# RWKV units that prepare both quarters ahead of the chain: what moves in a hybrid decoder step

## The chip, the cores and the metric

The kernel runs on one core of a Trainium2 chip. The metric is the device time of one execution in microseconds (us). Before the change it is 1862.17 us, the median of three runs (1860.52 to 1864.99). A difference under 0.2%, about 4 us, can't be told from no change.

## The reference, cut to what matters

One decoder layer runs for a prompt of 1024 tokens and for 8 samples of 8 tokens, 1088 columns in all; the model width is 1024. All is fp32. `h = RMSNorm(x)` is projected by one wide matrix; its columns feed sliding-window attention (branch A), RWKV-7 time mixing (branch B), two SiLU gates and two sigmoid merge gates. Each branch is gated and projected, the two are merged, projected again and added to `x`, and a last RMSNorm follows. Branch B is a recurrence over tokens, for 16 heads of 64:

```python
def step(S, inp):
    rt, wt, kt, vt, at, bt = inp
    sa = jnp.einsum('bhvk,bhk->bhv', S, at)
    S = S * wt[:, :, None, :] + sa[..., None] * bt[:, :, None, :] + vt[..., None] * kt[:, :, None, :]
    return S, jnp.einsum('bhvk,bhk->bhv', S, rt)
# r receptance, w decay = exp(-exp(-softplus(-(w0 + tanh(wl) @ w2)) - 0.5)), k key, v value,
# a = -kk (removal key), b = kk * sigmoid(a0 + al @ a2), kk = normalised k * k_k
```

Its output is normalised per head, gets the bonus `sum(r * k * r_k) * v`, and is gated.

## The kernel before

**Dense tiles.** The 93 weight tiles of 1024x128 are matrices of fp32 split into two fp32r parts (hi and lo). A dense tile is three products (hi by hi, hi by lo, lo by hi) over 8 row blocks and 3 column chunks (364, 364, 360), 72 matmuls that all have line L110 in the profile. PSUM results leave by ACT, DVE and POOL, most to DRAM.

**Stages.** `start` norms `x` and does the first three tiles (low-rank input, first gate, first key tile); PE, SP and POOL keep the program's order there. `rwkv` runs branch B with 56 dense tiles as filler; only PE's order is kept by hand there, the other engines' order is set by a scheduler with priorities (chain 400000, fronts 200000, inversion 0). `attention` and `final` follow.

**Order by a planner.** `drive` holds several streams, each a generator whose steps issue instructions. A stream yields how long it wants to wait on the planner's clock, counted in us of PE work, or the name of a mark that another stream sets. The stream that is due first goes next, and dense tiles, which never wait, fill the rest. So PE's order is fixed when the program is built. Due times are constants: WI (38.0) from the end of a front to its merge, WD (3.5) from a prefetch to its matmuls, WB from there to the bonus, WA ahead of later scores, WM, WH and WS in merge and chain.

**RWKV units.** Branch B is cut into 16 units: 4 pairs of head groups (two heads each), and 4 quarters of 256 tokens, the last with the 64 sample columns too. Within a quarter there are 4 chunks of 64 tokens. A unit `s` passes through:

- `front(s)`: for each of two groups `prefetch` (loads, L578) and `quarter` (L597): low-rank matmuls `lo`, decays `Pp` and their inverse (L650 to L653), normalised keys `kkn`, the products `RA` (receptances and removal keys, L669, L670) and `KB` (L678), the bonus (L682 to L688). The first group then waits for the mark `c{s-2}`, since some tiles have two buffers. Copies of `RA` go to `am` (DVE, L728) and `r0` (ACT, L729), the score matmuls `A` follow, then masked copies, `ab`, and transposes of `KB` and `zv`. The second group starts only then.
- `invert` (L764): the triangular systems go through DRAM to `TM`, and 31 steps of two DVE operations (`Tt` L784, `TR` L786) invert 32x32 blocks.
- `merge(s)` (matmuls `q_`): waits for `f{s}` plus WI, for the chain `c{s-1}` and the post `p{s-2}`; it fills the single tile `ti`.
- `chain(s)`: for each chunk three dependent matmul steps (PSUM tile `c`), whose results are copied half by ACT and half by DVE (`xs` L860 and L861, `vsu` L865 and L866), and the state update L877.
- `posts` and `samples` use what the chain leaves.

Of the kernel before, what the change touches and what calls it, by code (L numbers as in the profile page):

```python
# [14 lines left out]
P = 128  # L15
# [9 lines left out]
HD = 64  # L25
# [15 lines left out]
WI, WD, WB, WA, WM, WH, WS, WP, WT = 38.0, 3.5, 15.0, 0.8, 5.0, 1.4, 2.4, 5.0, 10.0  # L41
# [40 lines left out]
class Prog:  # L82
# [162 lines left out]
    def run(self):  # L245
        tc, nc = self.tc, self.nc
        nc.scalar.preload_act_table_set("natural_log_exp_and_others")
        with ExitStack() as top:
# [13 lines left out]
            self.d_l = dt([P, 2, NT], F32, name="d_l")  # L262
            self.d_s = [dt([P, NT], F32, name=f"d_s{m}") for m in range(NQS)]
# [17 lines left out]
    def start(self, xp, w0):  # L281

        nc, ep, prm, prd = self.nc, self.ep, self.prm, self.prd
        ones = xp.tile([P, P], F32, name="ones")
# [96 lines left out]
        go(tg)  # L381
        go(tk)
# [88 lines left out]
    def lora(self, c0, c1, z):  # L471
        nc, ep = self.nc, self.ep
        n = c1 - c0
        t = ep.tile([P, 364], F32, tag="zz", name=f"tl{c0}", bufs=2)
        self.sig_neg(t[0:64, :n], t[0:64, :n], z[0:64, :n], -2.0, 0.0)
        nc.vector.tensor_scalar(t[0:64, :n], t[0:64, :n], 2.0, -1.0, ALU.mult, ALU.add)
        zs = ep.tile([P, 2, 364], F32R, tag="zl", name=f"zs{c0}", bufs=1)
        for j, src in enumerate((t[0:64, :n], z[64:128, :n])):
            hi, lo = (slice(0, 64), slice(64, 128))[::1 - 2 * j]
            nc.scalar.activation(zs[hi, j, :n], src, AF.Copy)  # L480
            nc.vector.tensor_tensor(zs[lo, j, :n], src, zs[hi, j, :n].bitcast(F32), ALU.subtract)
        nc.sync.dma_start(self.d_l[:, :, c0:c1], zs[:, :, :n].bitcast(F32))

    def rwkv(self):
# [71 lines left out]
    def front(self, s):  # L556
# [16 lines left out]
        self.mark(f"f{s}")  # L573

# [3 lines left out]
    def prefetch(self, g, q):  # L578
# [3 lines left out]
        if g % 2 == 0:  # L582
            self.zl = ep.tile([P, 2, 364], F32R, tag="zl", name=f"zl{nm}", bufs=1)
# [8 lines left out]
        kkn = ep.tile([P, 320], F32, tag="kkn", name=f"kkn_{nm}", bufs=1)  # L592
# [4 lines left out]
    def quarter(self, g, q, gi, f):  # L597
# [9 lines left out]
        def v64(t):  # L607
            return t[:, :256].rearrange("p (c s) -> p c s", c=4)

        def s64(t):  # L610
            return t[:, 256:320].rearrange("p (b s) -> p b s", b=NB)

        def d64(t, off, w=64):
            return t[:, :260].rearrange("p (c s) -> p c s", c=4)[:, :, off:off + w]

        def d8(t, off, w=8):
            return t[:, 260:332].rearrange("p (b s) -> p b s", b=NB)[:, :, off:off + w]

# [4 lines left out]
        zr, zv = E("zr"), ep.tile([P, 5, 2, HD], F32, tag="zv", name=f"zv_{nm}", bufs=1)  # L623
# [7 lines left out]
        for j in range(2):  # L631
            t = E("e1", 2)
            ps = pl[j]
            self.mm(ps[:, :n], lhsT=w2[0][:, j, :], rhs=self.zl[:, j, :n], start=True, stop=False)
            self.mm(ps[:, :n], lhsT=w2[1][:, j, :], rhs=self.zl[:, j, :n], start=False, stop=True)
# [6 lines left out]
        nc.vector.memset(d64(sg, 0, 1), 0.0)  # L642
        nc.scalar.activation(d64(sg, 1), v64(res[0]), AF.Exp, scale=-1.0)
        if smp:
            nc.vector.memset(d8(sg, 0, 1), 0.0)
            nc.scalar.activation(d8(sg, 1), s64(res[0]), AF.Exp, scale=-1.0)
# [4 lines left out]
        Pp = E("Pp", 1, 332)  # L651
# [12 lines left out]
        RA = ep.tile([P, 5, 2, HD], F32, tag="RA", name=f"RA{nm}", bufs=1)  # L664
        KB = ep.tile([P, 5, 2, HD], F32, tag="KB", name=f"KB{nm}", bufs=1)

        def o8(t, j):
            return t[:, 4, j, :].rearrange("p (b s) -> p b s", b=NB)
        nc.vector.tensor_tensor(RA[:, :4, 0, :], v64(zr), d64(Pp, 1), ALU.mult)  # L669
        nc.vector.scalar_tensor_tensor(RA[:, :4, 1, :], v64(kkn), -1.0, d64(Pp, 0), ALU.mult, ALU.mult)  # L670
        if smp:
            nc.vector.tensor_tensor(o8(RA, 0), s64(zr), d8(Pp, 1), ALU.mult)
            nc.vector.scalar_tensor_tensor(o8(RA, 1), s64(kkn), -1.0, d8(Pp, 0), ALU.mult, ALU.mult)

        halves = [slice(h * 64, h * 64 + 64) for h in range(2)]
        for h, hr in enumerate(halves):
            for t, j in ((aa, h), (kf, 1 - h)):
                nc.vector.tensor_tensor(KB[hr, :4, j, :], v64(t)[hr], d64(Pi, 1)[hr], ALU.mult)  # L678
                if smp:
                    nc.vector.tensor_tensor(o8(KB, j)[hr], s64(t)[hr], d8(Pi, 1)[hr], ALU.mult)  # L680

        nc.vector.scalar_tensor_tensor(zr[:, :n], zr[:, :n], self.par(Q_RK + g), kf[:, :n], ALU.mult, ALU.mult)  # L682
        parts = self.split(ep, zr[:, :n], n, f"b{nm}")
        yield None, WB, "m"
        ps = self.ps("m", f"bo{nm}")
        self.sum2(ps[:, :n], self.bone, parts)
        nc.vector.tensor_tensor(zr[:, :n].rearrange("p (c s) -> p c s", s=64), ps[:, :n].rearrange("p (c s) -> p c s", s=64), zv[:, :n // 64, 0, :], ALU.mult)
        nc.sync.dma_start(self.d_b[g][:, a0:a0 + n], zr[:, :n])  # L688
        gn, qn = (g + 1, q) if gi == 0 else (g - 1, q + 1) if q < 3 else (g + 1, 0)
        if gn < NG and self.zmark(gn, qn) in self.marks:  # L690
            self.prefetch(gn, qn)

        if gi == 0:
            if f["s"] > 1:
                yield f"c{f['s'] - 2}", 0.0
            f["ab"] = cp.tile([P, f["nh"], HD], F32, tag="ab", name=f"ab{nm}", bufs=2, padded_shape=[P, 10, HD])
            f["vsu"] = cp.tile([P, 4, 2, P], F32, tag="vsu", name=f"vsu{nm}", bufs=2)
            f["pc"] = cp.tile([P, 4, 2], F32, tag="pc", name=f"pc{nm}", bufs=2)
            self.mark(f"v{f['s']}")
        if smp and f["s"] > 4:  # L700
            yield f"p{f['s'] - 4}", 0.0
        ab = f["ab"]
        S = dict(am=cp.tile([P, 2, 4, 2, HD], F32, tag="am", name=f"am{nm}", bufs=4),
                 r0=self.r0s[2 * (f["s"] % 2) + gi], ti=self.ti[:, gi],
                 kbt=cp.tile([P, 4, P], F32, tag="kbt", name=f"kbt{nm}", bufs=4),
                 vsu=f["vsu"][:, :, gi, :])
        sets = [(S, 0, 4, 4 * gi)]
# [799 lines left out]
```

## Time and profile before

| | |
|---|---|
| median of three runs | 1862.17 us |
| the profiled execution | 1868.65 us |
| its span, first to last instruction | 1866.9 us |
| mean granted TensorE clock | 0.951 |
| busy: PE, weight load, DVE, ACT, POOL | 89%, 84%, 65%, 52%, 27% |

The span is what one execution took from its first instruction to its last. Busy times are unions of an engine's instructions; two engines can be busy at once, so they don't add up. The granted clock is TensorE's, as a share of full speed. A wait is idle time of an engine, put down to what ended it.

### The profile page before, as it was taken

Reading aid. Unit: us, or ns where it says so; the run is one execution under the profiler, and the core shown is the slowest. Engines: PE = TensorE matmul, PEld = TensorE weight load, DVE = VectorE, ACT = ScalarE, POOL = GpSimd, SP = SyncE. Lnnn points to the kernel's source line nnn. Section 1 sums busy time; section 2 is a strip of 40 time slices with the busy share of each in tenths; the row PEclk is TensorE's granted clock in tenths of the full one; section 3 lists DMA queues with packets and bytes.
Section 4 is the critical chain, followed back from the end, with each engine's and each line's share of the span. In section 5 each row is a group of like instructions: output and inputs, shape, how many; then the busy total and the mean of one; then the engine's idle time right before and its main releaser. Section 6 shows DMA issues by size and latency. Waiting matters only on the chain.

```text
span 1866.9 us, 33535 instructions
## 1 busy us (share of the span) xinstructions
PE 1662.3 (89%) x11744; PEld 1568.0 (84%) x11744; DVE 1213.3 (65%) x3563; ACT 965.9 (52%) x2494; POOL 498.9 (27%) x650
## 2 busy tenths in 40 slices
PE   5889889799788897898898898898799999999997
PEld 4889789788778896787898788897699899899997
DVE  6323767767766876869767868855466777554443
ACT  5445547446456574466576467453466765432332
POOL 5554334244244234324432223231200000000000
PEclk9999999899889998999999899999799999999999
DMA  4334334334334333233343244322521445374521
GB/s 165 125 94 123 97 104 118 102 92 119 93 97 112 97 113 107 83 104 113 95 127 113 81 110 132 96 83 69 159 75 57 125 126 151 107 240 139 191 90 60
DMA packets 208812, 209.32 MB, mean 112 GB/s; under 512 B 108452, under 2 KB 179732, under 8 KB 208612
## 3 DMA queue, kind: packets, MB, share of 16 engines
q1 hardware_dynamic: 193860, 157.03, 28.9%
q0 software_dynamic: 14784, 50.15, 8.4%
q8 instruction: 93, 1.52, 0.4%
q14 instruction: 75, 0.61, 0.1%
HBM read 144.01 MB, written 65.07 MB: 112 GB/s over the span
## 4 chain that ended last, share of the span: by engine, by line
PE 53%; DVE 25%; ACT 6%; DMA 6%; issue 5%; POOL 3%; SPq 1%; DVEq 0%; POOLq 0%; ACTq 0%
PE d L110 32%; DVE TR L786 6%; PE wo L110 5%; DVE Tt L784 5%; PE c L110 3%; DVE KB L678 2%; PE s L110 2%; PE o L110 2%; DVE vsu L877 2%; PE pt L108 1%; PE y L110 1%; PE A L110 1%; DMA TM<-s 1%; POOL wlo L171 1%; DMA wraw<-in_w 1%
## 5 line engine op out<-in xcount | busy, mean ns | idle before, releaser
L110 PE MATMUL d<-hhi,whi 128*128 128x364 f32 (+1 forms) x1656 | 585.7, 354 | 69.5 <-ACT zz L404 21.4
L110 PE MATMUL d<-hlo,whi 128*128 128x364 f32 (+1 forms) x1656 | 566.6, 342 | 7.9 <-DVE hlo L350 7.0
L110 PEld LDWEIGHTS d<-hhi,whi 128*128 128x128 f32 x1656 | 329.7, 199 | 83.0 <-ACT zz L404 23.8
L110 PEld LDWEIGHTS d<-hlo,whi 128*128 128x128 f32 x1656 | 329.7, 199 | 12.7 <-DVE hlo L350 9.6
L110 PE MATMUL d<-hhi,wlo 128*128 128x364 f32 (+1 forms) x1656 | 333.0, 339 | 0.0
L110 PEld LDWEIGHTS d<-hhi,wlo 128*128 128x128 f32 x1656 | 283.4, 194 | 2.6 <-issue 2.1
L171 POOL TENSOR_TENSOR wlo<-wraw,whi 128x1024 fp32r<-128x1024 f32 x56 | 135.4, 2418 | 199.5 <-PE d L110 90.4
L786 DVE TENSOR_TENSOR TR<-TR,Tt 96x90 f32<-96x90 f32 (+26 forms) x496 | 149.5, 302 | 11.9
L784 DVE TENSOR_TENSOR Tt<-TM,TR 96x90 f32<-96x90 f32 (+26 forms) x496 | 136.4, 275 | 14.9 <-DMA TM<-s 3.3
L170 ACT ACTIVATE whi<-wraw 128x1024 fp32r<-128x1024 f32 x90 | 95.1, 1057 | 80.0 <-PE d L110 52.6
L853 POOL TENSOR_TENSOR sp<-vsu,pc 64x128 f32<-64x128 f32 x128 | 55.9, 437 | 224.6 <-DVE vsu L877 218.9
L405 POOL TENSOR_TENSOR zz<-zz,pad 128x364 f32<-128x364 f32 (+1 forms) x75 | 73.4, 979 | 133.5 <-ACT zz L404 118.6
L1341 POOL TENSOR_TENSOR xr<-xr,frs 128x256 f32<-128x256 f32 x2 | 1.8, 933 | 342.1 <-ACT frs L1338 342.1
L877 DVE SCALAR_TENSOR_TENSOR vsu<-c,pc,sp 64x64 f32<-64x64 f32 x240 | 68.0, 283 | 16.9 <-PE c L110 12.3
L1080 ACT ACTIVATE sc<-sc,st 128x256 f32<-128x256 f32 (+1 forms) x128 | 62.1, 488 | 28.9 <-DVE st L1076 28.8
L678 DVE TENSOR_TENSOR KB<-e,sg 64x256 f32<-64x256 f32 x128 | 64.2, 512 | 1.2
L403 ACT ACTIVATE pad<-d,prm 128x364 f32<-128x364 f32 (+1 forms) x75 | 40.7, 543 | 45.8 <-PE d L110 39.1
L110 PEld LDWEIGHTS c<-xs,ti 128*128 128x128 f32 x256 | 38.4, 205 | 30.8 <-DVE xs L861 28.4
L110 PE MATMUL d<-yhi,whi 128*128 128x364 f32 (+1 forms) x192 | 63.9, 333 | 0.0
L110 PE MATMUL d<-ylo,whi 128*128 128x364 f32 (+1 forms) x192 | 63.8, 332 | 0.0
L110 PE MATMUL d<-oh,whi 128*128 128x364 f32 (+1 forms) x192 | 63.2, 329 | 0.0
L110 PE MATMUL d<-ol,whi 128*128 128x364 f32 (+1 forms) x192 | 62.9, 328 | 0.0
(334 smaller groups left out, 3686.8 us busy)
## 6 DMA issues: line engine op xcount, KB each, us to landing
wraw<-in_w POOLq DMA_DIRECT2D x56, 512.0 KB, 4.0
wraw<-in_w SPq DMA_DIRECT2D x37, 512.0 KB
d_z<-zz POOLq DMA_DIRECT2D x48, 182.0 KB, 2.3
zv<-d_z SPq DMA_DIRECT2D x48, 128.0 KB
d_m<-sp SPq DMA_DIRECT2D x32, 182.0 KB
TM<-s SPq DMA_DIRECT2D x72, 64.0 KB
stageo<-d_o SPq DMA_DIRECT2D x8, 544.0 KB
d_z<-zz POOLq DMA_DIRECT2D x24, 180.0 KB, 3.9
```

The costliest lines, as they stand in the source:

```text
L108: self.nc.tensor.transpose(out, lhsT, rhs)
L110: self.nc.tensor.matmul(out, lhsT=lhsT, rhs=rhs, **kw)
L170: nc.scalar.activation(hi, raw, AF.Copy)
L171: (nc.vector if self.dve_lo else nc.gpsimd).tensor_tensor(lo, raw, hi.bitcast(F32), ALU.subtract)
L403: nc.scalar.activation(pad[:, 1:1 + m], ps[:, :m], AF.Copy, scale=mu)
L405: nc.gpsimd.tensor_tensor(z[:, :m], z[:, :m], pad[:, 0:m], ALU.add)
L678: nc.vector.tensor_tensor(KB[hr, :4, j, :], v64(t)[hr], d64(Pi, 1)[hr], ALU.mult)
L784: nc.vector.tensor_tensor(tv, M[s // 16][:np_, s % 16:s % 16 + 1, s + 1:32].to_broadcast([np_, cc, w]), R[:np_, 0:cc, s:s + 1].to_broadcas ...
L786: nc.vector.tensor_tensor(R[:np_, 0:cc, s + 1:32], R[:np_, 0:cc, s + 1:32], tv, ALU.add)
L853: nc.gpsimd.tensor_tensor(sp[h], vsu[h, c, :, h], pc[h, c].unsqueeze(2).to_broadcast([64, 2, HD]), ALU.mult)
L877: nc.vector.scalar_tensor_tensor(dst, pn[h, i, h], pc[h, c, i:i + 1], sp[h, i], ALU.mult, ALU.add)
L1080: nc.scalar.activation(sc[k], sc[k], AF.Exp, bias=st[:, 0, k:k + 1], accum_out=st[:, 1, k:k + 1])
```

## The change

The wait for `c{s-2}` moves from the middle of the front to behind the preparation of both groups. `quarter` ends with `KB`; `bonus`, `arrays`, `scores` and `turn` become functions of their own, and bonus and transposes run behind the inversion's issue. Receptances and removal keys are written straight into a persistent tile `X` (four of them), from which scores and chain read, so that the copies to `am` and `r0` go. Split low-rank factors are made once in `start` and kept in DRAM (`d_c`); `lora` writes its two parts from two smaller tiles, by two DMAs. `TM`'s second half is narrower. The chain's copies are all on DVE. Planner constants: WB 15.0 to 4.0, WA 0.8 to 2.0, new WR 3.0 and WE 12.0. Tiles `xs` and `sp` of the chain have one buffer in place of two.

```diff
-WI, WD, WB, WA, WM, WH, WS, WP, WT = 38.0, 3.5, 15.0, 0.8, 5.0, 1.4, 2.4, 5.0, 10.0
+WI, WD, WB, WA, WM, WH, WS, WP, WT, WR, WE = 38.0, 3.5, 4.0, 2.0, 5.0, 1.4, 2.4, 5.0, 10.0, 3.0, 12.0
 ...  # start()
         self.pre[T_RKVG] = self.load_w(T_RKVG)
         go(tg)
+        for g in range(NG):
+            raw, hi, lo = (xp.tile([P, 364], F32, tag="sq", name=f"l{x}{g}", bufs=4)[:, :2 * P] for x in "rhl")
+            nc.sync.dma_start(raw, self.I["lora"][:, g].rearrange("p j c -> p (j c)"))
+            nc.scalar.activation(hi.bitcast(F32R), raw, AF.Copy)
+            nc.vector.tensor_tensor(lo.bitcast(F32R), raw, hi, ALU.subtract)
+            for x, t in enumerate((hi, lo)):
+                nc.sync.dma_start(self.d_c[:, g, x], t)
         go(tk)
 ...  # rwkv()
-        self.r0s = [cp.tile([P, 2, 4, HD], F32, name=f"r0{x}") for x in range(4)]
+        self.xs = [cp.tile([P, 4, 4, HD], F32, name=f"X{x}") for x in range(4)]
 ...  # front()
         for i in range(2):
             yield from self.quarter(2 * p + i, q, i, f)
+        self.mark(f"e{s}")
+        yield f"e{s}", WE
+        if s > 1:
+            yield f"c{s - 2}", 0.0
+        if q == 3 and s > 4:
+            yield f"p{s - 4}", 0.0
+        f["ab"] = ...   # and vsu, pc
+        self.mark(f"v{s}")
+        for i in range(2):
+            self.arrays(2 * p + i, q, i, f)
+        for i in range(2):
+            yield from self.scores(2 * p + i, q, i, f)
 ...  # s1 to DRAM
         with self.tc.high_priority(offset=INV):
             self.invert(nm, n2, f)
         self.mark(f"f{s}")
+        for i in range(2):
+            yield from self.bonus(2 * p + i, q, f["q"][i])
+            yield from self.turn(2 * p + i, q, f["q"][i])
+        self.mark(f"t{s}")
+        ...   # prefetch of the next unit's first quarter
 ...  # prefetch()
-        raw = ep.tile([P, 2, P], F32, tag="w2", name=f"w2_{nm}", bufs=1)
-        nc.sync.dma_start(raw, self.I["lora"][:, g])
-        w2 = [ep.tile([P, 2, P], F32R, tag=f"w2{x}", name=f"w2{x}_{nm}", bufs=1) for x in "hl"]
+        w2 = ep.tile([P, 2, 2, P], F32R, tag="w2", name=f"w2_{nm}", bufs=1)
+        nc.sync.dma_start(w2.bitcast(F32).rearrange("p x j c -> p x (j c)"), self.d_c[:, g])
-        nc.scalar.activation(w2[0], raw, AF.Copy)
-        nc.vector.tensor_tensor(w2[1], raw, w2[0].bitcast(F32), ALU.subtract)
 ...  # quarter(): zr, zv, kkn, Pp and KB get two buffers
-        nc.vector.tensor_tensor(RA[:, :4, 0, :], v64(zr), d64(Pp, 1), ALU.mult)
-        nc.vector.scalar_tensor_tensor(RA[:, :4, 1, :], v64(kkn), -1.0, d64(Pp, 0), ALU.mult, ALU.mult)
 ...  # after the bonus
-        if gi == 0:
-            if f["s"] > 1:
-                yield f"c{f['s'] - 2}", 0.0
-                nc.vector.tensor_copy(am[hr, 1, :, h], RA[hr, :4, 1, :])
-                nc.scalar.activation(X["r0"][hr, h], RA[hr, :4, 0, :], AF.Copy)
 ...  # the new functions, cut
+    def bonus(self, g, q, S):
+        parts = self.split(ep, zk[:, :n], n, f"b{g}_{q}")
+        yield None, WB if g % 2 else 0.0, "m"
+        ...   # sum2, times zv, d_b
+    def arrays(self, g, q, gi, f):
+        X = self.xs[2 * (f["s"] % 2) + gi]
+        for h, hr in enumerate(halves):
+            nc.vector.tensor_tensor(X[hr, :, h], self.v64(zr)[hr], self.d64(Pp, 1)[hr], ALU.mult)
+            nc.vector.scalar_tensor_tensor(X[hr, :, 2 + h], self.v64(kkn)[hr], -1.0, self.d64(Pp, 0)[hr], ALU.mult, ALU.mult)
+    def scores(self, g, q, gi, f):
+            yield WA if c0 or gi else WR
+            ...   # A matmuls, rhs X[hr, c, h::2, :]; ab first, then the masked copies
+    def turn(self, g, q, S):
+        ...   # the transposes of KB and zv, as before
 ...  # invert(): the second half of M holds 16 columns in place of 32
 ...  # chain()
+        yield f"t{s}", WH
         yield f"m{s}", WH
-            nc.scalar.activation(xs[hs[0]], px[hs[0], :, hs[0]], AF.Copy)
-            nc.vector.tensor_copy(xs[hs[1]], px[hs[1], :, hs[1]])
+            for h in hs:
+                nc.vector.tensor_copy(xs[h], px[h, :, h])
-            nc.scalar.activation(vsu[hs[0], c, :, hs[0]], pu[hs[0]], AF.Copy)
-            nc.vector.tensor_copy(vsu[hs[1], c, :, hs[1]], pu[hs[1]])
+            for h in hs:
+                nc.vector.tensor_copy(vsu[h, c, :, h], pu[h])
```

## Rows read from the trace of the kernel before

**Rows 1.** Busy time by stretch: us of each engine with instructions, granted clock, DMA.
```profile
200.00:1290.00 1090.00, 948.72 (x7105) 897.37 (x7105) 805.78 (x2461) 605.81 (x1611) 373.59 (x494) 0.94 0.37 104
1290.00:1340.00 50.00, 33.92 (x179) 28.17 (x178) 23.32 (x56) 18.06 (x46) 15.60 (x22) 0.74 0.31 91
1340.00:1867.00 527.00, 514.87 (x3542) 489.90 (x3540) 303.89 (x874) 242.00 (x606) 8.13 (x8) 0.99 0.40 126
```

**Rows 2.** Chain of work that ended last, whole span: shares by line.
```profile
PE d L110 32%; DVE TR L786 6%; PE wo L110 5%; DVE Tt L784 5%; PE c L110 3%; DVE KB L678 2%; PE s L110 2%; PE o L110 2%; DVE vsu L877 2%; PE pt L108 1%; PE y L110 1%; PE A L110 1%; DMA TM<-s 1%; POOL wlo L171 1%; DMA wraw<-in_w 1%
```

**Rows 3.** Timeline of unit 9 (start us, us, engine, line, operation): its steps only.
```profile
786.53 1.16 PE L110 MATMUL A<-RA,KB 64*128 64x128 f32 x16
...
817.93 1.16 PE L110 MATMUL A<-RA,KB 64*128 64x128 f32 x16
...
833.25 0.19 DVE L786 TENSOR_TENSOR TR<-TR,Tt 96x31 f32<-96x31 f32 x1
...
866.78 2.60 SPq L788 DMA_DIRECT2D s<-TR  x3
...
879.47 0.86 PE L110 MATMUL q_1a<-ab 32*32 32x32 f32 x32
...
884.41 0.61 PE L110 MATMUL c<-vsu,am 128*128 128x128 f32 x4
...
926.79 1.16 PE L110 MATMUL A<-RA,KB 64*128 64x128 f32 x16
```

**Rows 4.** PE's waits, 100 to 1320 us: total us, times, longest.
```profile
PE c L110 <- DVE xs L861: 22.3, 15, 4.0
PE d L110 <- ACT zz L404: 19.2, 7, 4.5
PE d L110 <- DVE gz L435: 17.0, 4, 8.8
PE c L110 <- DVE vsu L866: 15.7, 18, 2.6
PE d L110 <- ACT sho L414: 10.5, 6, 2.8
```

**Rows 5.** DVE groups, 200 to 1290 us: busy us, mean ns, idle before.
```profile
L861 DVE COPY xs<-c 64x128 f32<-64x128 f32 x60 | 17.7, 295 | 48.2 <-ACT xs L860 47.0
...
L866 DVE COPY vsu<-c 64x128 f32<-64x128 f32 x60 | 17.7, 295 | 23.9 <-ACT vsu L865 22.5
```

**Rows 6.** Single lines: ns of one, minimum, median and maximum.
```profile
L678 DVE TENSOR_TENSOR KB<-e,sg x128: 406/418/2823, 123.6 to 1221.0; 64x256 f32<-64x256 f32 x128
...
L728 DVE COPY am<-RA x64: 274/291/2944, 126.9 to 1224.8; 64x256 f32<-64x256 f32 x64
...
L729 ACT ACTIVATE r<-RA x64: 401/416/422, 123.3 to 1217.5; 64x256 f32<-64x256 f32 x64
...
L860 ACT ACTIVATE xs<-c x64: 253/272/274, 249.1 to 1313.3; 64x128 f32<-64x128 f32 x64
...
L590 ACT ACTIVATE w2h<-w x32: 399/403/419, 3.5 to 1167.5; 128x256 fp32r<-128x256 f32 x32
```

**Rows 7.** Start, timeline of SP, then ACT and PE.
```profile
73.98 0.33 SPq L436 DMA_DIRECT2D d_g<-gz  x1
...
75.08 0.60 SPq L584 DMA_DIRECT2D zl<-d_l  x1
...
76.85 0.48 SPq L455 DMA_DIRECT2D out_sk<-sp  x1
...
84.92 0.57 ACT L404 ACTIVATE zz<-d,prd 128x364 f32<-128x364 f32 x1 [2.06 <-DMA out_sk<-sp]
...
89.13 0.43 PE L110 MATMUL d<-hhi,whi 128*128 128x364 f32 x1 [2.92 <-ACT whi L170]
```

**Rows 8.** Pieces of the chain that ended last: start us, us, what.
```profile
0.75 2.75 DMA w<-in_lora
...
1334.61 4.49 DMA vT<-d_v
```

More of the change, by code (lines that the diff above doesn't have):

```diff
@@ L573, in front, with v64, s64, d64 @@
         self.mark(f"f{s}")
+        for i in range(2):
+            yield from self.bonus(2 * p + i, q, f["q"][i])
+            yield from self.turn(2 * p + i, q, f["q"][i])
+        self.mark(f"t{s}")
+        gn, qn = (2 * p, q + 1) if q < 3 else (2 * p + 2, 0)
+        if gn < NG and self.zmark(gn, qn) in self.marks:
+            self.prefetch(gn, qn)
+    @staticmethod
+    def v64(t):
+        return t[:, :256].rearrange("p (c s) -> p c s", c=4)
+    @staticmethod
+    def s64(t):
+        return t[:, 256:320].rearrange("p (b s) -> p b s", b=NB)
+    @staticmethod
+    def d64(t, off, w=64):
+        return t[:, :260].rearrange("p (c s) -> p c s", c=4)[:, :, off:off + w]
+    @staticmethod
+    def d8(t, off, w=8):
+        return t[:, 260:332].rearrange("p (b s) -> p b s", b=NB)[:, :, off:off + w]
+    @staticmethod
+    def o8(t, j):
+        return t[:, 4, j, :].rearrange("p (b s) -> p b s", b=NB)
     def zmark(self, g, q):
@@ L703, in quarter @@
[L703 to L707, printed above, removed]
+                    nc.vector.tensor_tensor(self.o8(KB, j)[hr], self.s64(t)[hr], self.d8(Pi, 1)[hr], ALU.mult)
+        nc.vector.scalar_tensor_tensor(zk[:, :n], zr[:, :n], self.par(Q_RK + g), kf[:, :n], ALU.mult, ALU.mult)
@@ L749, in quarter @@
                     nc.scalar.activation(abv, pv[hr, :cn, 64:128], AF.Copy)
+            for h, hr in enumerate(halves):
+                pv, vr = pvs[h], halves[1 - h]
+                am0 = S["smp"]["am"][:, 0, :, h] if c0 else S["am"][:, :, h]
+                am1 = S["smp"]["am"][vr, 1, :, h] if c0 else S["X"][vr, :, 2 + h]
+                nc.vector.tensor_tensor(am0, pv[:, :cn, 0:64], self.cst(mi, 64).unsqueeze(1).to_broadcast([P, cn, 64]), ALU.mult)
+                nc.vector.tensor_tensor(am1, pv[vr, :cn, 64:128],
+                                        self.cst(ms, 64, vr.start, vr.stop).unsqueeze(1).to_broadcast([64, cn, 64]), ALU.mult)
+    def turn(self, g, q, S):
+        nc = self.nc
+        nm = f"{g}_{q}"
+        ident = self.cst(C_ID, P)
+        halves = [slice(h * 64, h * 64 + 64) for h in range(2)]
+        sets = [(S, 0, 4)] + ([(S["smp"], 4, 1)] if q == 3 else [])
+        for Y, c0, cn in sets:
             yield None, 0.0, "m"
@@ L771, in invert @@
         np_ = 3 * nb
-        M = [ep.tile([P, 16, 32], F32, tag=f"TM{x}", name=f"TM{x}{nm}", bufs=1) for x in range(2)]
+        M = [ep.tile([P, 16, 32 - 16 * x], F32, tag=f"TM{x}", name=f"TM{x}{nm}", bufs=1) for x in range(2)]
         R = ep.tile([P, 11, 32], F32, tag="TR", name=f"TR{nm}", bufs=1)
@@ L870, in chain @@
             for i in range(2):
-                self.mm(psy[:, c % 2, i, :], lhsT=vsu[:, c, i, :], rhs=Q[i]["am"][:, 0, c].rearrange("p h s -> p (h s)"), start=False, stop=(c % 2 == 1 and i == 1))
+                self.mm(psy[:, c % 2, i, :], lhsT=vsu[:, c, i, :], rhs=Q[i]["am"][:, c].rearrange("p h s -> p (h s)"), start=False, stop=(c % 2 == 1 and i == 1))
             if c == 3 and not smp:
```

147 lines of the change are left out of this document (67 added, 80 removed).

## The prediction, as it went on record

> **What bounds the kernel now.** I read the busy time by stretch first [rows 1]. From 200 to 1290 us, the RWKV stage with dense tiles as filler, PE is busy 948.7 of 1090 us at a granted clock of 0.94; from 1340 on it is busy 514.9 of 527 at 0.99. The second stretch has little left to win. In the first, PE stands for 1090 - 948.7 = 141 us, and the clock takes about 948.7 x 0.06 = 57 us of the work: 198 us lost. Between them lie 50 us (1290 to 1340) with PE at 33.9 and a clock of 0.74: that is 33.9 x 0.74 = 25 us of work, so 25 us lost. The granted clock has two levels (1.2 and 2.4 GHz), and the three rows order it as they order PE's share of busy time: 0.74, 0.94, 0.99. So a wait of PE costs more than its own length.
>
> The chain of waits [rows 2] shows what the stage hangs on besides dense matmuls: the inversion on DVE (TR 6% and Tt 5% of the span). The timeline of one unit [rows 3] shows the loop these shares come from; its steps recur in all 16 units. The scores of the unit's first quarter start at 786.53, straight behind the matmuls of the chain two units back. Those of the second quarter start at 817.93: in between, the whole second quarter is prepared. The inversion runs from 833.25 to 866.78, the merge starts at 879.47, the chain at 884.41, and at 926.79 the next-but-one unit begins. The loop of two units is 140.3 us, and 817.93 + 1.16 - 786.53 = 32.6 of it lie between the two score blocks' ends.
>
> But PE follows an order written at build time, and dense tiles fill it. A shorter loop is worth only the time in which PE stands or is slow. So I also read who PE waits for [rows 4]: the chain's two copies (22.3 + 15.7 = 38.0 us) and, apart from the loop, the evacuation of dense tiles (19.2 + 17.0 + 10.5 = 46.7).
>
> **The change part by part.** The sum is made against the profiled execution's own 1868.65 us (span 1866.9), which lies 6.5 above the median of the runs, 1862.17.
>
> *Both quarters ahead of the wait (loop).* Behind the chain two units back now come only the products for both quarters: 8 of 64x256 on DVE at 0.418 [rows 6] = 3.3 us, then two score blocks of 1.16 with about 2 us around them: about 8 us where 32.6 stood. The loop falls from 140.3 to about 116, 17%. The PE work in it is 140.3 x (948.7 x 0.94 / 1090 = 0.82) = 115 us. So the new loop would be just as long as PE's own work, and PE could not run without any loss; not all of it comes back. Of the 198 us lost, 38 belong to the chain's copies and 47 to dense evacuation; 113 are left, the clock's share included. I take 40 us, a third of that; bounds 0 (dense work fills it anyway) and -113.
>
> *Chain's copies, all on DVE.* ACT copies one half and DVE the other, one behind the other: DVE stands 47.0 + 22.5 us for ACT before its own copy [rows 5]. One hop between engines goes, and 128 more copies of 0.295 = 38 us are laid on DVE, less than the 69.5 us that it stands today. I take half of PE's 38.0 us: -19. Bounds: -38, and +38 if each added copy stood on the path in full.
>
> *Dense evacuation.* ACT loses 128 copies of 0.272 = 35 us, 64 of 0.416 = 27 (r0), 24 of 0.403 = 10 (w2h) [rows 6]: 72 of 605.8 us in the stage [rows 1], 12%. I take 12% of the 46.7 us: -6; bounds 0 and -47.
>
> *Arrays.* The eight products per unit replace four of 128x256 and four copies of 0.291 [rows 6]; at the same 0.418 for a product (estimate: DVE's time follows the columns, 256 in both) that is 3.3 against 2.8 us, nothing on PE. Narrowing the second half of TM takes bytes from three of six loads; 0.
>
> *The tail.* With a shorter loop the RWKV units end while dense tiles are left, and the stretch 1290 to 1340 fills up. Of its 25 us I take 20, since the first load of the attention stage (4.49 us [rows 8]) still ends a wait. Bounds 0 and -25.
>
> *New waits.* (a) The score matmuls come 3 planned us (WR) behind the chain, the products take 3.3 on DVE after a queue: 1 us per unit, +16. (b) The second quarter's prefetch now stands 3.5 planned us (WD) ahead of its matmuls, and its two factors arrive in one load; the nearest load, of half the bytes, took 2.75 us [rows 8], so I take 0. Behind either wait stand all dense matmuls, in PE's order. Together +16; bounds 0 and +105 (the second rival).
>
> *The split of the low-rank factors, moved to the start.* This part speaks against the change. In program order SP gets 24 DMAs between the last gate DMA (73.98) and the spill's last three (the last at 76.85) [rows 7]. SP is one of the engines whose order is kept by hand there. For each of 8 groups it issues a load, then waits for ACT's copy and DVE's difference before it issues the two stores. A load took 2.75 us from issue to landing [rows 8], the copy 0.403, the difference about the same, two issues about 0.34 each (as the gate's 0.33): 2.75 + 0.40 + 0.42 + 0.68 = 4.2 us, 34 us in all. The spill's stores move from 76 to about 108. A zz buffer hangs on them: today ACT waits for out_sk's landing at 84.92 and PE stands until 89.13. After, PE would stand from about 86 to 112, 26 less the 2.9 that it stands today: 23; I take +22, since weights then lie ready behind it. Bounds: 0 (zl, a later DMA, passes at 75.08, so SP's order is not rigid for all) and +33.
>
> [...]
>
> Sum: -40 - 19 - 6 - 20 + 16 + 22 = -47; 1868.65 - 47 = 1821.7 for a profiled execution, and 6.5 less for the median: 1815.
>
> **The rivals.**
> *The loop turns into PE's time in full.* For it: the first scores follow the chain at once, so no other wait ends later there. PE then recovers 100 of the 113 us and no new wait shows: 1868.65 - 100 - 19 - 6 - 20 + 22 = 1745.7, or 1739. Against: DVE is busy 805.8 of 1090 us [rows 1], and in an 11% shorter stage it would be at 83%.
>
> *The inversion is late (slower).* The inversion has the lowest priority on DVE and will run beside the preparation of two quarters of the next unit in place of one; and the merge's mark now comes ahead of the transposes, while its planned distance of 38 us (WI) stays. One quarter's DVE work is 4 products of 0.418 at least and some ten operations of the same width: about 6 us. From scores to merge the trace has 879.47 - 817.93 = 61.5 us, against 38 + 5 planned. It decides from the point where the inverse lands later than PE's order puts the merge; then PE stands in front of it, with all dense matmuls behind. If that is 6.6 us in each unit, +105 take the place of the -40 and the +16: 1868.65 + 105 - 19 - 6 - 20 + 22 = 1950.7; since the merge also waits for the chain of the unit before (the code's second condition), part of it would be hidden; I price it at half, +53: 1898.7, or 1892. Against: where that chain ends last, the inversion has time to spare.
>
> *The loop is hidden anyway.* Dense tiles fill PE whatever the loop does; the named waits alone change: 1868.65 - 19 - 6 - 20 + 16 + 22 = 1861.7, or 1855. For it: the longest of PE's named waits are not for the inversion [rows 4].
>
> **How the numbers follow.** Forecast 0.50, full gain 0.17, inversion late 0.20, hidden 0.13. A difference under 0.2% (4 us) can't be told from none here. Forecast and full gain are faster but for 0.02 of the forecast that may end level; of the hidden case 0.07 is faster, 0.05 level and 0.01 slower. Faster 0.48 + 0.17 + 0.07 = 0.72; same 0.02 + 0.05 = 0.07; slower 0.20 + 0.01 = 0.21. The forecast's own range is 1785 to 1845. For 8 in 10 it reaches half into the outer rivals: 1745 to 1885.
>
> **What would show it.** Loop: the two score blocks of a unit a few us apart, and the same step two units on about 116 us later. Copies: no DVE wait for ACT at xs and vsu, PE's waits for them halved. Tail: no stretch with PE near 34 of 50 us between the stages. Start: SP with 24 DMAs in a row from 74 us, and PE standing for over 20 us at about 86. New waits: PE waiting for DVE's X ahead of the scores. The prediction fails if PE waits for the merge's operands in most units, if the granted clock in the stage falls below 0.94, or if PE is busy over 95% of it.

## The result, and the profile after

The changed kernel takes **1926.91 us** (median of four runs, 1925.88 to 1931.61), beside 1862.04 us for the kernel before: a ratio of **1.0351, 95% interval 1.0330 to 1.0373**. It is 65 us slower where 47 faster were forecast, and outside the range. The profiled execution takes 1925.88 us, 57.2 more than that of before.

Busy time by stretch of the changed kernel, columns as in [rows 1]:

```profile
100.00:150.00 50.00, 18.67 (x98) 18.36 (x99) 3.60 (x12) 11.11 (x26) 22.79 (x38) 0.66 0.38 122
200.00:1290.00 1090.00, 909.84 (x6753) 856.49 (x6754) 830.51 (x2563) 543.82 (x1390) 376.44 (x491) 0.91 0.37 101
1290.00:1340.00 50.00, 49.25 (x424) 47.07 (x423) 22.73 (x67) 17.37 (x43) 18.38 (x21) 1.00 0.33 99
1340.00:1924.00 584.00, 569.88 (x3871) 542.97 (x3869) 324.50 (x910) 269.68 (x659) 25.80 (x26) 0.99 0.41 128
```

The stretch between the stages is full: 49.25 x 1.00 us of work where [rows 1] had 33.9 x 0.74, so 24 us. Two places are lost: the start (PE at 18.67 of 50 us, against 44.84 before) and the RWKV stage (909.8 at 0.91, where [rows 1] had 948.7 at 0.94). The same stretch of the start in the kernel before:

```profile
100.00:150.00 50.00, 44.84 (x272) 43.63 (x271) 12.12 (x39) 21.98 (x56) 26.48 (x32) 0.97 0.34 101
```

The prediction's own sign of failure, a granted clock under 0.94 in the stage, has come up.

PE's waits of the changed kernel from 100 to 1400 us, as in [rows 4]:

```profile
PE d L110 <- DVE gz L444: 45.6, 6, 16.5
PE d L110 <- ACT whi L170: 38.8, 1, 38.8
PE c L110 <- DVE xs L910: 24.6, 17, 3.2
PE d L110 <- ACT sho L423: 20.3, 7, 10.4
PE c L110 <- DVE vsu L915: 20.3, 21, 3.3
...
PE A L110 <- DVE X L788: 8.6, 9, 3.8
PE lo L110 <- DMA w<-d_c: 6.8, 3, 4.4
```

There is a single wait of 38.8 us for weights in the start. The gate's product `gz` stands at 45.6 us where [rows 4] had 17.0. The waits for the chain's copies, all on DVE now, are no shorter than in [rows 4] (44.9 against 38.0).

The start of the changed kernel, to set beside [rows 7]: SP, then POOL, ACT and PE.

```profile
78.88 0.38 SPq L386 DMA_DIRECT2D lr<-in_lora  x1
...
115.90 0.33 SPq L390 DMA_DIRECT2D d_c<-ll  x1
...
117.92 0.14 POOL L754 MEMSET ams<- 64x64 f32 x1 [36.25 <-DMA d_c<-ll]
...
123.84 0.57 POOL L169 DMA_DIRECT2D wraw<-in_w  x1
...
128.40 1.06 ACT L170 ACTIVATE whi<-wraw 128x1024 fp32r<-128x1024 f32 x1 [2.46 <-DMA wraw<-in_w]
...
129.51 0.67 PE L110 MATMUL d<-hhi,whi 128*128 128x364 f32 x1 [38.81 <-ACT whi L170]
```

The block of 24 DMAs lasts 37 us (78.88 to 116.23), where 34 were worked out. The row to learn from is POOL's: its memset of `ams`, a tile of the next stage, waits 36.25 us for a store of the block to land. I read it so that this tile takes over memory of the block; e1, e2 and e5 below bear it out. POOL keeps the program's order, so the next weight load (123.84) stands behind the memset, and PE behind that.

Units 8 to 11 of the changed kernel, PE but for one row of the chain's last step (of unit 8); beside [rows 3]:

```profile
884.41 1.18 DVE L926 SCALAR_TENSOR_TENSOR vsu<-c,pc,sp 64x64 f32<-64x64 f32 x4
...
915.09 1.16 PE L110 MATMUL A<-X,KB 64*128 64x128 f32 x16
918.52 1.18 PE L110 MATMUL A<-X,KB 64*128 64x128 f32 x16
...
947.38 1.41 PE L110 MATMUL lo<-zl,w 128*128 128x320 f32 x4
...
980.87 1.16 PE L110 MATMUL A<-X,KB 64*128 64x128 f32 x16
```

The two score blocks of unit 10 lie 3.4 us apart, as meant. But they start 29.5 us after the chain two units back has ended (884.41 + 1.18), so that chain no longer sets them. What does is the front itself: 33.5 us from `lo` (947.38) to the scores, and 32.3 from the scores of one unit to the `lo` of the next, 65.8 in all. The fronts are one stream, so no part of it overlaps the next front. The last state update of all units (last start in these rows) comes 26.6 us later than before, first the kernel before, then the changed one:

```profile
L877 DVE SCALAR_TENSOR_TENSOR so<-c,pc,sp x16: 275/284/291, 495.3 to 1318.6; 64x64 f32<-64x64 f32 x16
```

```profile
L926 DVE SCALAR_TENSOR_TENSOR so<-c,pc,sp x16: 266/284/293, 523.2 to 1345.2; 64x64 f32<-64x64 f32 x16
```

One stretch of DVE ahead of those scores (start, length, operation), with ACT's last step for the gate, and PE at its end:

```profile
887.63 0.41 DVE L711 TENSOR_TENSOR KB<-e,sg 64x256 f32<-64x256 f32 x1
...
887.76 0.49 ACT L222 ACTIVATE gz<-gz 128x364 f32<-128x364 f32 x1
...
893.23 0.41 DVE L740 TENSOR_TENSOR X<-zr,Pp 64x256 f32<-64x256 f32 x1
...
897.22 1.52 DVE L711 TENSOR_TENSOR KB<-e,sg 64x256 f32<-64x256 f32 x4
...
900.73 0.53 DVE L444 TENSOR_TENSOR gz<-d,gz 128x364 f32<-128x364 f32 x1
...
901.32 0.67 PE L110 MATMUL d<-hhi,whi 128*128 128x364 f32 x1 [14.78 <-DVE gz L444]
```

From 884 to 900 DVE runs without a break: keys and products of both quarters (fronts have priority 200000), and between them the last steps of an inversion. The gate's product (dense, priority 0) is ready when ACT is done at 888.25 and runs at 900.73. The kernel gives dense tiles two PSUM buffers, so PE stands for 14.78 us. The Trainium skill says that the queues of ScalarE, VectorE and GpSimdE are strict FIFO ("PSUM — Partial Sum Buffer", section "Engine vs sequencer instructions"). This trace agrees: the product is served 12.5 us after it is ready, in the order that was built, though PE waits.

### The profile page after: what moved, and what is told of

The parts are those of the page before. It is cut to its first block, busy times and chain, and to the rows that moved or that the text cites. A ratio compares the mean times of both kernels' runs of the same rounds, so it can differ in the third digit from the quotient of the medians.

```text
span 1924.1 us, 33459 instructions
## 1 busy us (share of the span) xinstructions
PE 1665.7 (87%) x11744; PEld 1570.1 (82%) x11744; DVE 1239.1 (64%) x3667; ACT 911.9 (47%) x2270; POOL 510.8 (27%) x654
## 4 chain that ended last, share of the span: by engine, by line
PE 48%; DVE 27%; DMA 8%; issue 7%; ACT 4%; POOL 3%; SPq 2%; DVEq 0%; POOLq 0%; ACTq 0%
PE d L110 29%; DVE Tt L832 6%; DVE TR L834 5%; PE wo L110 5%; PE c L110 2%; DVE vsu L926 2%; PE s L110 2%; DVE KB L711 2%; PE A L110 2%; PE o L110 2%; DMA wraw<-in_w 2%; PE pt L108 1%; DMA TM<-s 1%; PE y L110 1%; DMA lr<-in_lora 1%
## 5 line engine op out<-in xcount | busy, mean ns | idle before, releaser
L110 PE MATMUL d<-hhi,wlo 128*128 128x364 f32 (+1 forms) x1656 | 339.4, 343 | 0.0
L110 PEld LDWEIGHTS d<-hhi,wlo 128*128 128x128 f32 x1656 | 287.5, 197 | 3.9 <-issue 2.9
L832 DVE TENSOR_TENSOR Tt<-TM,TR 96x90 f32<-96x90 f32 (+26 forms) x496 | 157.1, 317 | 23.1 <-DMA TM<-s 10.2
L834 DVE TENSOR_TENSOR TR<-TR,Tt 96x90 f32<-96x90 f32 (+26 forms) x496 | 135.6, 273 | 12.7
L902 POOL TENSOR_TENSOR sp<-vsu,pc 64x128 f32<-64x128 f32 x128 | 63.2, 494 | 236.8 <-DVE vsu L926 218.6
L110 PEld LDWEIGHTS c<-vsu,kbt 128*128 128x128 f32 x256 | 37.7, 202 | 30.0 <-DVE vsu L915 29.3
```

Source lines behind the costliest of these rows:

```text
L110: self.nc.tensor.matmul(out, lhsT=lhsT, rhs=rhs, **kw)
L832: nc.vector.tensor_tensor(tv, M[s // 16][:np_, s % 16:s % 16 + 1, s + 1 - 16 * (s // 16):].to_broadcast([np_, cc, w]), R[:np_, 0:cc, s:s + ...
L834: nc.vector.tensor_tensor(R[:np_, 0:cc, s + 1:32], R[:np_, 0:cc, s + 1:32], tv, ALU.add)
L902: nc.gpsimd.tensor_tensor(sp[h], vsu[h, c, :, h], pc[h, c].unsqueeze(2).to_broadcast([64, 2, HD]), ALU.mult)
```

## The experiments

Ratios are against runs of the kernel before, made beside each experiment. "The three-undone kernel" is e6.

**e1: the block in one piece.** One load, one copy, one difference, two stores over all 8 groups.

```diff
-        for g in range(NG):
-            raw, hi, lo = (xp.tile([P, 364], F32, tag="sq", ..., bufs=4)[:, :2 * P] for x in "rhl")
+        raw, hi, lo = (xp.tile([P, KT, 364], F32, tag="xt", ..., bufs=3)[:, :, :2 * P] for x in "rhl")
```

> The kernel after, with the split of the low-rank factors in the start done once over all 8 groups (one load, one ACT copy, one DVE difference, two stores) in place of 8 times in turn. Theory A (the block of 24 DMAs costs the start's 39 us): PE's stand of 38.8 us before 129.5 us falls to some 8, and the time to 1890 to 1897. Rival (the start's delay is made up later by dense work that waits anyway, all of the loss lies in the RWKV stage): 1915 to 1927.

Measured 1911.33 us, 1.0263 (1.0243 to 1.0282): 15.6 less. PE's stand falls from 38.8 to 17.2 us, not to 8, and the time lies above the theory's range. The stand is the block's, but POOL still waits 15.0 us for its last store.

**e2: the same 24 DMAs behind the key tile's stores.** It moves the block past the spill's stores, on which the prediction's route (SP, then a `zz` buffer) hung.

> The kernel after, with the same 24 DMAs behind the last key tile's stores in the program, so that these stores no longer wait on SP. If PE's stand of 38.8 us comes through SP and the held zz buffer, as the prediction had it, it falls below 12 us and the time to about 1895. If it comes through POOL, whose memsets of later tiles wait for the block's memory and hold the weight loads behind them, it stays over 30 us and the time at 1920 to 1927.

Measured 1930.42 us (one run), and PE stands as long as before. The rows of POOL and PE:

```profile
118.85 0.14 POOL L754 MEMSET ams<- 64x64 f32 x1 [36.21 <-DMA d_c<-ll]
...
PE d L110 <- ACT whi L170: 39.1, 1, 39.1
```

The stores that the predicted route hung on no longer wait for the block, and the stand stays: that route is refuted. The route through the memory and POOL holds.

**e5: the block early.** One load behind the first chunk's norm; copy, difference (in place) and stores behind the second's.

> The changed kernel, with the low-rank factors' block done once over all 8 groups and early in the start: one load behind the first chunk's norm, one ACT copy, one DVE difference and two stores behind the second chunk's norm, so that its memory is free before POOL's memsets ask for it. Theory (the block costs what PE stands for at about 129 us, because POOL's memsets of later tiles wait for the block's memory and hold back the weight loads behind them): the stand of 38.8 us goes nearly whole (under 5 us left), and the time falls by 33 to 39 us, to 1888 to 1894. Rival (the work itself is the cost, wherever it stands in the start, because ACT, DVE and SP are on the path there): the stand is gone but the start is late by 10 to 20 us in smaller waits, 1898 to 1908.

Measured 1890.77 us, 1.0146 (1.0125 to 1.0167): **36.1 us** less, PE's stand 2.5 us, and POOL's memset of `ams` comes without a wait:

```profile
81.32 0.14 POOL L754 MEMSET ams<- 64x64 f32 x1
...
PE d L110 <- ACT whi L170: 2.5, 1, 2.5
```

Of the 36.1 us, e1 had 15.6 by the one piece alone; the rest is the place. The block's work itself is hidden there.

**e3: the gate's evacuation first.**

```diff
+            with self.tc.high_priority(offset=300000):
-            self.sig_neg(t, t, ps, -1.0, 0.0)
+                self.sig_neg(t, t, ps, -1.0, 0.0)
```

(and the product behind it)

> The kernel after, with the gate tiles' evacuation (three ACT steps, one DVE product) at a priority above the fronts. Theory B (the two quarters' preparation stands in one block on DVE ahead of the dense evacuation, and PE runs out of PSUM buffers): PE's waits for gz fall from 45.6 us to under 15 and the time to 1885 to 1900, clock included. Rival (DVE is simply too full: the same time comes back as waits for the merge or the chain): waits move, 1920 to 1930.

Measured 1904.25 us, 1.0224 (1.0195 to 1.0254): **22.7 us** less, and PE's waits for `gz` fall from 45.6 us to one of 3.0. Half of that shows in the time.

**e4: the kernel before with the chain's copies all on DVE.**

```diff
-            nc.scalar.activation(xs[hs[0]], px[hs[0], :, hs[0]], AF.Copy)
-            nc.vector.tensor_copy(xs[hs[1]], px[hs[1], :, hs[1]])
+            for h in hs:
+                nc.vector.tensor_copy(xs[h], px[h, :, h])
```

(and the same for `vsu`)

> The kernel before with one part of the change alone: the chain's copies of xs and vsu all on DVE. The prediction's step (one hop less, PE's waits of 38 us halved): 1840 to 1856. Rival C (128 more copies on a DVE that the loop hangs on cost the RWKV stage its loss): 1875 to 1895.

Measured 1881.21 us, 1.0107 (1.0081 to 1.0134): **19 us slower** by itself. Its waits of PE, 100 to 1400 us, beside [rows 4]:

```profile
PE c L110 <- DVE xs L861: 22.6, 14, 3.5
...
PE ss_b L110 <- DVE sx L900: 14.7, 5, 5.6
...
PE q_1a L110 <- DVE ab L808: 8.5, 6, 2.6
PE c L110 <- DVE vsu L866: 7.1, 12, 1.6
```

`vsu` gains 8.6 us and `xs` nothing, so the copies' waits fall from 38.0 to 29.7, the way that was forecast. But waits grow where other work needs DVE: `sx` of the samples from 5.9 to 14.7, `ab` ahead of the merge's matmuls from 5.8 to 15.4 in all. DVE's busy time from 200 to 1290 us rises from the 805.8 of [rows 1] to 834.8, and the last state update moves from 1318.6 to 1329.2. The listed waits grow by 9 us in sum; where the rest of the 19 goes isn't shown.

**e6: three undone.** Early block, gate first, copies back on ACT and DVE, in the changed kernel. **e7: gate first in the kernel before.** **e8: e6 with all dense evacuations first.**

> The changed kernel with the three suspected costs undone together: the early block of the run before, the gate's evacuation at high priority, and the chain's copies back on ACT and DVE. What is left of the change is the order of the quarters, the products in one persistent tile and the tail. Theory (three separate costs, which add): 1926.9 - 38 - 22.7 - 19 = 1847, in a range of 1840 to 1856, so the moved quarters are worth some 15 us against the kernel before. Rival (the moved quarters themselves lose, since the fronts have become serial and the DVE burst delays more than the gate): 1862 or more, with waits of PE left at the other dense evacuations and at the products ahead of the scores.

> The kernel before, with the gate's evacuation at high priority alone. It tells whether the -22.7 us of that edit in the changed kernel mends something that the change broke or something that was there. Theory (the burst of both quarters broke it; before, PE waited 17.0 us for the gate's product and at most a few us at once): 1852 to 1860, so at most 10 us. Rival (the gate's place in DVE's queue was a fault of the kernel before as well): 1840 to 1848, and then the three-undone kernel owes its gain to this and not to the moved quarters.

> The three-undone kernel with all dense evacuations at high priority, not the gate's alone. Theory (DVE's burst of both quarters also holds up the small DVE steps of the shift's and the spill's evacuations, on which ACT and then PE wait, 10.4 us at one place): the waits of PE for sho, pad, zz and sp fall by 15 to 25 us and the time by as much against the three-undone kernel, to 1825 to 1835. Rival (DVE is the engine with no slack, so what the evacuations gain the chain and the inversion lose): within 5 us of the three-undone kernel.

e6: 1862.26 us, 0.9989 (0.9976 to 1.0002), not the 1847 of the sum. e7: 1856.81 us, 0.9964 (0.9951 to 0.9977). e8: 1866.25 us, 1.0009 (0.9990 to 1.0027): the waits for `sho` go (24.8 to 0.6 us) and others grow, among them 14.1 us for weights in the start, so it says little on the stage; the time is within its rival's 5 us of e6. Where e6 stands against the kernel before, from the stretches 600 to 1000 and 1290 to 1400 us, first before, then e6:

```profile
600.00:1000.00 400.00, 347.54 (x2569) 328.57 (x2568) 307.73 (x922) 233.25 (x626) 145.44 (x195) 0.94 0.37 106
1290.00:1400.00 110.00, 93.62 (x586) 85.77 (x586) 61.23 (x183) 52.00 (x141) 15.60 (x22) 0.86 0.34 102
```

```profile
600.00:1000.00 400.00, 335.65 (x2497) 313.45 (x2496) 303.52 (x910) 213.19 (x575) 140.09 (x190) 0.90 0.36 101
1290.00:1400.00 110.00, 108.42 (x722) 104.62 (x720) 53.35 (x158) 58.82 (x144) 14.65 (x16) 1.00 0.42 128
```

In us of work at the full clock: the tail wins 108.4 - 93.62 x 0.86 = 28, the middle loses 347.54 x 0.94 - 335.65 x 0.90 = 25. The units do end earlier in e6 (last state update at 1284.8, where it was 1318.6), but PE has less done by then. What is left of the change (order, tile, factors, later bonus) is worth nothing as it stands.

**e9, e11, e13: the old order of the quarters in the new code**, in e6 (e9; e13 with 15 planned us behind each quarter) and in the changed kernel (e11).

```diff
-        for i in range(2):
-            yield from self.quarter(2 * p + i, q, i, f)
+        yield from self.quarter(2 * p, q, 0, f)
         ...  # WE goes; wait for c{s-2}, then for each i:
+            if i:
+                yield from self.quarter(2 * p + 1, q, 1, f)
             self.arrays(2 * p + i, q, i, f)
             yield from self.scores(2 * p + i, q, i, f)
```

> The three-undone kernel (1862.3 us) with the order of the quarters as before the change too: first quarter, wait for the chain two units back, its scores, then the second quarter and its scores. Products in the persistent tile, the early block and the gate's priority stay. What is left against the kernel before with the gate's priority (1856.8) is the tile, the prepared factors and the later bonus. Theory (the moved quarters win some 25 us in the tail and lose as much in the middle of the stage through a burst on DVE, so they are worth nothing): within 8 us of the three-undone kernel, 1854 to 1866, with PE's waits for the chain's copies down from 57.2 to about 40 us, the clock from 600 to 1000 us up from 0.90 to about 0.94, and the tail loss back. Rival (the moved quarters gain and the tile or the factors lose): 1870 or more.

> The changed kernel with nothing but the order of the quarters as before; the block in the start, the copies on DVE and the gate's low priority stay. Theory (the burst is what makes the gate late, so without it the 45.6 us of PE's waits for the gate's product fall to about the 17 us of the kernel before): 1900 to 1912, i.e. the order costs 15 to 25 us in this surrounding though it costs nothing in the three-undone kernel. Rival (the order is worth the same everywhere, nothing): 1922 to 1932.

> The order of the quarters as before, put back properly: in the run before, the scores followed their quarter's preparation after only 3 planned us, where the kernel before has 15 planned us and the bonus between, and PE stood 120 us for the products and keys. Here 15 planned us stand behind each quarter's preparation; all else as in the three-undone kernel. Theory (the moved quarters win the tail and lose the middle, so they are worth nothing): 1854 to 1870, PE's wait for the products under 25 us, the score blocks some 30 us apart, the tail loss back, 600 to 1000 us at a clock of 0.93 or more. Rival (the moved quarters are worth a good deal and the persistent tile or the later bonus lose it): 1880 or more.

All three are far slower: 1965.98 (1.0554, 1.0531 to 1.0578), 2014.81 (1.0820) and 1952.63 us (1.0489). The theories missed, and the rivals' ranges hold (for e9 and e13) by number alone, since these kernels don't undo one thing. In e9 and e11 the scores stand right behind their quarter, and PE waits 93.5 and 90.3 us for `X`; in e13 the two distances of 15 lengthen the front, PE waits 69 us for `ab`, the units end at 1403 us, and PE is busy 60.6 of the 110 us of the tail. What the order is worth by itself stays open; the package of order, tile, factors and later bonus is e6 against e7, +5.5 us.

**e10, e12, e14: the quarters spread**, in e6, with planned us between them (the edit) and behind them (WE, 12 in e6).

```diff
         for i in range(2):
+            if i:
+                yield 12.0
             yield from self.quarter(2 * p + i, q, i, f)
```

> The three-undone kernel with the two quarters' preparation spread: 12 planned us of other work between the first quarter and the second, and 6 in place of 12 behind the second. Theory (it is the burst of two quarters on DVE that costs the middle of the stage): PE's waits for xs, vsu and sho (82 us together) fall by 10 to 25 us, the time to 1840 to 1855. Rival (DVE's sum of work is what counts, and not how it is bunched): within 5 us of 1862, with the waits only moved.

> As the spread kernel before (12 planned us between the quarters and 6 behind the second: 1872.3), with 6 and 6, so that the planned length of a unit is that of the three-undone kernel (0 and 12). There the middle of the stage had gained (600 to 1000 us: PE 367 us busy at 0.94, against 336 at 0.90), while the units ended 45 us later and the tail was lost again. Theory (the burst costs the middle, the longer loop costs the tail, so half the spread at the same planned length keeps both): units end by 1300 us, PE waits for xs and vsu under 50 us, 1840 to 1855. Rival (what one gives the other takes, at any spread): 1858 to 1870.

> 8 planned us between the quarters and 3 behind the second. By the theory of a burst, the products follow the second quarter too soon and PE waits for them (15 us or more at the scores), 1850 to 1862; by the rival (the sum alone counts), the loop is 1 planned us a unit shorter and the time within 5 us of the run with 6 and 6.

12 and 6: 1872.33 us (1.0058). 6 and 6: 1874.10 (1.0069). 8 and 3: 1880.87 (1.0109). The first gains the middle (600 to 1000 us: 366.99 at 0.94) and loses the tail (87.37 of 110 at 0.82); the second keeps the tail, but PE's waits for the copies rise from 57.2 to 68.8 us; in the third those for `ab` rise to 43.9. None of the three lies in its theory's range or in its rival's: all are slower than either. The first does show that the front's planned length sets the units: 6 planned us more in each, and the last state update moves from 1284.8 to 1329.4. No spread paid; what the burst costs by itself stays open.

**e15, e16: the chain's copies all on ACT**, in e6 and in e7; the mirror of e4.

```diff
-            nc.scalar.activation(xs[hs[0]], px[hs[0], :, hs[0]], AF.Copy)
-            nc.vector.tensor_copy(xs[hs[1]], px[hs[1], :, hs[1]])
+            for h in hs:
+                nc.scalar.activation(xs[h], px[h, :, h], AF.Copy)
```

> The three-undone kernel (1862.3) with the chain's copies all on ACT: the mirror of the changed kernel's edit, which had laid them all on DVE. DVE loses 128 copies of some 0.3 us (38 us of about 815), ACT gains 128 of 0.27 (35 us of about 575). Theory (DVE is where every wait of PE in the stage begins, whatever the order and the priorities, so only less work on DVE shortens it): PE's waits for xs and vsu fall from 57 to under 40 us, the others do not grow, 1840 to 1854. Rival (the chain waits for a hop and a place in a queue, and ACT's queue is no better, so the copies are worth the same on either): 1858 to 1870, with PE's waits for xs and vsu named for ACT and as long as before.

> The kernel before with the gate's evacuation at high priority (1856.8) and the chain's copies all on ACT. Theory (less work on DVE): 1836 to 1850, a version better than both kernels. Rival: 1853 to 1865. If this kernel gains as much as the three-undone one does, the moved quarters stay worth nothing; if it gains less, the moved quarters were held back by DVE alone.

e15: **1834.98 us, 0.9848** (0.9828 to 0.9869). e16: 1845.27 us, 0.9904 (0.9885 to 0.9922). So the edit gives 27 us with the moved quarters and 12 without, and the package, worth +5.5 us before, is now worth -10. PE's waits for the chain in e6, then in e15 (L927 is the state update, still on DVE; L916 the copy):

```profile
PE c L110 <- DVE xs L911: 28.7, 22, 3.3
PE c L110 <- DVE vsu L916: 28.5, 28, 4.1
```

```profile
PE c L110 <- DVE vsu L927: 15.0, 9, 3.3
...
PE c L110 <- ACT vsu L916: 7.2, 5, 3.2
```

**e17, e18: other work off DVE**, in e6 (copies left) and in e15.

```diff
-        nc.vector.tensor_scalar(kf[:, :n], aa[:, :n], self.par(Q_KA + g), self.prd[:, 41 + g:42 + g], ALU.mult, ALU.add)
+        nc.scalar.activation(kf[:, :n], aa[:, :n], AF.Identity, scale=self.par(Q_KA + g), bias=self.prd[:, 41 + g:42 + g])
...
-        nc.vector.tensor_copy(y, ps)
+        nc.scalar.activation(y, ps, AF.Copy)
```

> The three-undone kernel (1862.3) with other work taken off DVE and the chain's copies left as they are, on ACT and DVE: one factor of the keys (32 operations of 0.41 us) and the copy of the group norm's centred values (32 of 0.43) go to ACT, 27 us in all, where the copies were 38. Theory (DVE's load sets PE's waits, whatever is taken off it): 27/38 of the 27.3 us that the copies gave, 1838 to 1852, with the waits for xs and vsu under 45 us. Rival (the copies gained by their own place, ahead in ACT's queue instead of behind DVE's preparation): within 6 us of 1862, with the waits for xs and vsu as long as before, over 50 us.

> Both: the chain's copies all on ACT, and those two operations too. Theory (load): another 10 to 20 us below the 1835.0 of the copies alone, 1815 to 1826. Rival (place): 1830 to 1842, since the chain's copies now stand behind more work on ACT.

e17: 1862.71 us, 0.9998 (0.9983 to 1.0014), nothing; its waits for the copies are as long as in e6:

```profile
PE c L110 <- DVE xs L911: 29.9, 21, 3.2
PE c L110 <- DVE vsu L916: 27.0, 25, 4.0
```

So load as such was not the cause (my theory there fell). What e6's DVE does ahead of such a copy, in the longest of its waits for `xs` (PE's matmul ended at 1154.77):

```profile
1154.77 2.85 POOL L171 TENSOR_TENSOR wlo<-wraw,whi 128x1024 fp32r<-128x1024 f32 x1
...
1155.25 0.25 ACT L910 ACTIVATE xs<-c 64x128 f32<-64x128 f32 x1
1155.30 2.40 DVE L833 TENSOR_TENSOR Tt<-TM,TR 96x72 f32<-96x72 f32 x1
...
1159.74 0.30 DVE L911 COPY xs<-c 64x128 f32<-64x128 f32 x1
...
1160.09 0.69 PE L110 MATMUL c<-xs,ti 128*128 128x64 f32 x2 [3.33 <-DVE xs L911]
```

ACT copies its half 0.5 us later; DVE's half stands 4.5 us behind steps of an inversion and a front. Added up over e6's trace, 117 of the 165 us that DVE works between a matmul's end and its second copy are the inversion's `Tt` and `TR`, of which e17 took nothing away. From the matmul's end to the second copy's end it takes 1.89 us on average in e6 and 1.92 in e17, but 0.97 in e15; before, 1.78, and 1.50 in e4, where the copies got quicker and other work paid. So the copies' place in DVE's queue is what is left of the causes tried; no run changes that place and nothing else.

The row of `Tt` shows one thing more: it lasts 2.40 us, where the median `Tt` of e6 takes 0.23, and ends with POOL's split of a weight tile. In e6 51 DVE instructions between 150 and 1400 us are over 0.7 us longer than the median of their form, 79 us in sum, and each of them overlaps an elementwise operation of POOL. It was so before the change as well (54, 83 us), so it is not what the change lost, but it lengthens DVE's queue.

e18: **1818.88 us, 0.9768** (0.9746 to 0.9789): once the copies are out, less load does pay, 16 us. It is the fastest kernel here, 43 us under the kernel before. In its stage PE is at a clock of 0.95:

```profile
200.00:1290.00 1090.00, 967.66 (x7300) 918.02 (x7299) 772.96 (x2301) 657.24 (x1761) 394.24 (x513) 0.95 0.40 112
```

The last state updates of e6, e15 and e18:

```profile
L927 DVE SCALAR_TENSOR_TENSOR so<-c,pc,sp x16: 267/284/292, 474.1 to 1284.8; 64x64 f32<-64x64 f32 x16
```

```profile
L927 DVE SCALAR_TENSOR_TENSOR so<-c,pc,sp x16: 266/284/291, 468.5 to 1256.9; 64x64 f32<-64x64 f32 x16
```

```profile
L927 DVE SCALAR_TENSOR_TENSOR so<-c,pc,sp x16: 266/283/291, 465.7 to 1239.7; 64x64 f32<-64x64 f32 x16
```

The units end 27.9 us earlier, then 17.2 more, and the times fall by 27.3 and 16.1: here, unlike from the kernel before to e6, units that end earlier are worth their full length. In e17 the units end 1.0 us earlier, and the time stays.

## Why the prediction was wrong, step by step

- **Loop, -40: failed.** The step "behind the chain two units back now come only the products" held, but the forecast took a loop of 116 us from the one wait that was moved. The next bound was 65.8 us a unit of the front itself, two units 132, and I had not added up what a front does in a row. Over the last 14 units the chain's ends lie 134.0 us apart for two units (from 407 to 1345 us), against 138.3 before (351 to 1319): 3% in place of 17%. And PE did not gain from it: its work in the stage fell, by the terms below.
- **Copies, -19: wrong sign.** Alone, in the kernel before, they cost +19 (e4). I weighed the hop saved against DVE's idle time (38 us of work, less than 69.5 of idling), as if idle time were where the copies fall. The copies' own waits did fall, by 8 us, but the work behind them on DVE (samples, merge, state update) came later, and the sum had no term for it. The bound of +38 had held it.
- **Dense evacuation, -6: wrong sign.** Its three waits went from the 46.7 us of [rows 4] to 74.6 (45.6 + 20.3 + 8.7 for `zz`): the work left ACT, but the gate's product was queued on DVE behind two quarters. Worth 22.7 us (e3). I had moved work to DVE in two terms and never asked who stands behind it at a lower priority.
- **Start, +22: right place, wrong route, too small.** 36.1 us (e5), above its bound of +33. The block took 37 us where SP's sum said 34 (4.2 us a group held for all but the first). But it reached PE through memory that POOL's next memset needed (e2), with no buffer to soften it. The row of PE in [rows 7] had named it: the wait until 89.13 ended with the weights (`whi`, which waited for their load), and not with a `zz` buffer.
- **Tail, -20: the number right (24 us), by luck.** The reason was that the units end earlier. They end later, at 1345 in place of 1319; the stretch is full because the dense tiles were held up still more. In e6, with the units' end at 1285, it is full for the reason that was forecast.
- **New waits, +16: the sum right, its parts not.** PE waits 8.6 us for `X`, where 16 were forecast, and 6.8 for the factors' load ahead of `lo`, where 0 was.
- The slower rival, the late inversion, had the sign by another mechanism: waits for `ab` ahead of the merge grew only from 5.8 to 14.7 us. Its sum, like that of the hidden loop, also kept the tail's -20, for which the units would have to end earlier.

The three culprits add to 36.1 + 22.7 + 19 = 78 us when each is measured by itself (the copies in the kernel before, the others in the changed one), and to 65 together (e6). Why they don't add isn't shown; two of them lie in DVE's queue. With them undone the time is that of the kernel before.

Open: the order of the quarters by itself; the place of the copies in DVE's queue by itself; and the chain's tile `xs` with one buffer in place of two, which was not tried.

## What to carry to other kernels

Moving a wait shows the next one: before pricing it, add up the whole sequence that the wait stood in. Work moved to an engine with idle time is not free: ask which operations of lower priority stand behind it, and who waits for them; an operation in a dependent chain belongs on the engine whose queue is shortest when it becomes ready. And a transfer put at the end of a stage holds its memory until it lands, and so the first write of the next stage that needs this memory, with all that stands behind that write.

## What the runs showed that I had not expected

A copy of 64x128 out of PSUM takes 272 ns on ACT and 295 on DVE, nearly the same, yet all on ACT gives 27 us in e15 and 12 in e16, and all on DVE costs 19 (e4). The Trainium skill says that ScalarE sits closer to PSUM ("VectorE: DVE Perf Modes", section "Specifications"). The 23 ns agree. But 128 x 23 ns are 3 us, so the copy's own length did not make the difference.

Gains interact: the same two operations taken off DVE gave 0 us with the chain's copies on DVE (e17) and 16 without (e18).
